# Late hidden tiles' transfers on GpSimd's queue, and split-on-load operands loaded into their own place

## The chip, the cores and the metric

The kernel runs on one core of one Trainium2 chip. The core has five engines that run side by side, each with its own instruction queue: TensorE (PE, matrix products; PEld are its weight loads), VectorE (DVE), ScalarE (ACT), GpSimd (POOL) and SyncE (SP). An engine's queue is worked off in order. DMA transfers are issued from the queues of SP, ACT or POOL and carried out by the core's 16 DMA engines. The metric is the device time of one execution in microseconds (us), smaller is better; the program before takes 2143.97 us (median of 3 runs, 2143.37 to 2144.52).

## The reference

A small hybrid network with two layers over 1024 tokens of 1024 channels, all in fp32. Layer 0 mixes by retention and a gated delta rule, layer 1 by a gated linear recurrence; each layer then has the feed-forward part that the change is in:

```python
def conv_ffn(hn, w_up, conv_w, conv_b, w_down):
    up = causal_dwconv(hn @ w_up, conv_w) + conv_b
    gate, val = jnp.split(up, 2, axis=-1)
    return (jax.nn.silu(gate) * val) @ w_down
...
    for layer in range(DEPTH):
        hn = rms_norm(h, norm_mix[layer])
        ...
        h = h + conv_ffn(rms_norm(h, norm_ffn[layer]), ffn_w_up[layer], ffn_conv_w[layer],
                         ffn_conv_b[layer], ffn_w_down[layer])
    return rms_norm(h, norm_final)
```

The hidden width is 2816, that is 22 tiles of 128 channels, each with a gate and a value part. The convolution is over three tokens, channel by channel.

## The kernel before

**Precision.** PE multiplies a rounded fp32 format. To keep fp32 accuracy every operand is split into a high part (a cast by ScalarE) and a low part (the operand less its high part, by VectorE), and every product is three matmuls, `mm3` (L319 to L321): high by high, high by low, low by high. A weight quarter is 128x512, arrives in a `raw` tile (L292), and is split at L272 (cast, `whi`) and L273 (subtract, `wlo`). Some quarters are sums of others (L294 to L296, L309).

**Seven products for eight.** Pairs of tiles are multiplied by a scheme that needs seven products in place of eight, on sums and differences of blocks. A product (`pair_product`) is 4 blocks of 128 channels deep, so 12 matmuls of 128x128 by 128x512. Operand number o = 0 to 6 has its own place in SBUF, `operand(o)`: 0 to 2 in `s2` (printed as `s_4144` in layer 0), 3 to 6 in `s1` (`s_96`). A place holds the high and the low parts of 4 blocks of 128 channels by 512 tokens.

**First half of the feed-forward, `ffn(layer, gain)` (from L834).** For each of the 22 hidden tiles p, `pair_products` makes gate and value of the tile (seven products, results summed into `halo` at L810). `gate(p)` and `hidden(p)` then apply the convolution (L850 on ACT, two steps L852 on DVE for each of gate and value), the silu (L936) and the product (L941). The tile is needed as an operand of the second half, but the operand places are still in use; so `store_parts(p)` writes its seven operand parts to DRAM. Tiles are grouped by c: 0 to 7, 8 to 15, 16 to 21. Some parts are stored already split (high and low, L880, into `pf_dram`): operands {0, 1, 3} of the first group and {0, 1, 3, 5} of the others. The rest is stored whole (L881, L906, into `sf_dram`), 256 KB each. Tiles of the second half of a group need the tile four (or three) before: they read it back at L894 and L895. In layer 1 the tiles from 16 on are not put through this scheme; they are split at once and stored as two transfers of 512 KB (L870, into `lf_dram`).

**Second half (down-projection).** For c = 0, 1 (and 2 in layer 0), for t = 0 to 3 (256 output channels each), for o = 0 to 6: a product of a weight quarter with operand o of group c, and its eviction into `h` (L820). Group 2 has products of 3 blocks, 9 matmuls.

**Where the operands come from.** `load_set(c, o)` fills place o for group c. A stored-split operand is 8 direct loads (L914). A split-on-load operand is 4 loads of 128x512 (L922) into eight half tiles, its *room*: R and three of the general `t` tiles, used in turn. ACT casts each to the high part in the operand's place (L924), and DVE subtracts into the low part (L925). The sets of the first group are loaded in the course of tile 21's products (`after(21, o)`), each into a place that tile 21's product o has just been the last to read; those of the next group in the last output tile (t = 3) of the group before, by the tables `following` (layer 0) and `plain` (layer 1).

**What sets the order.** Only PE's order of the first two tiles is written by hand. Everything else is laid out per engine by the framework's scheduler from the program and the dependences between tiles. All transfers that are named above are issued by SP, in one order. SP has at most 8 transfers in flight; a transfer whose data or place isn't ready holds up all behind it.

Names for places below: T1 is the passage from tile 21 to group 0 (layer 0), T1' the same in layer 1, T2 from group 0 to group 1 in layer 0, T4 in layer 1, T3 from group 1 to group 2 (layer 0 alone).

Of the kernel before, what the change touches and what calls it, by code (L numbers as in the profile page):

```python
# [16 lines left out]
ALU = mybir.AluOpType  # L17
# [6 lines left out]
HALF = 512  # L24
# [65 lines left out]
def f32(ap):  # L90
    return ap.bitcast(F32)
# [12 lines left out]
class Block:  # L104
# [718 lines left out]
    def ffn(self, layer, gain):  # L823
        nc, I = self.nc, self.I
        V, A = nc.vector, nc.scalar
        third = gain is not None
        sets = 3 if third else 2
        y_dram = self.tc.dram_tile([NPAIR, P, T], F32, name=f"yf_dram{layer}")
        s_dram = self.tc.dram_tile([sets, 5, 4, P, HALF], F32, name=f"sf_dram{layer}")

        p_dram = self.tc.dram_tile([sets, 4, 4, 2, P, HALF], F32, name=f"pf_dram{layer}")
        if not third:
            l_dram = self.tc.dram_tile([NPAIR - 16, 2, P, T], F32, name=f"lf_dram{layer}")
        depth = lambda c: 4 if c < 2 else 3  # L834

        def where(c, o):

            if c == 0 or not third:
                return self.operand(o)
            if c == 1:  # L840
                return self.operand((o + 3) % 7)
            if o < 3:
                i = (20, 14, 26)[o]
                return self.slots1(i, 6).rearrange("p (s n c) -> p n s c", n=2, c=256)
            return self.s2[:, :, 6 * (o - 3):6 * (o - 2), :]
# [10 lines left out]
        blocks = lambda ap: ap.rearrange("p (n j c) -> p n j c", n=2, j=2)  # L856
        halves = lambda ap: ap.rearrange("p (n c) -> p n c", n=2)
        place = {1: 0, 4: 1, 2: 2, 6: 3, 5: 4}

        whole = [{0: 0, 1: 1, 3: 2}] + 2 * [{0: 0, 1: 1, 3: 2, 5: 3}]  # L860
        room, loads = {}, [0, 0, 0]

        def store_parts(p, y, hi):

            hi = hi.bitcast(F32R)
            lo = self.parts.tile([P, T], F32R, tag="lo", name="lo")
            if p >= 16 and not third:
                self.split_half(y, (hi, lo))
                for e, t in enumerate((hi, lo)):
                    nc.sync.dma_start(l_dram[p - 16, e], f32(t))  # L870
                return
            c, k = divmod(p, 8)
            kk = depth(c)
            first = slice(0, HALF)

            def store_split(o, src, at):
                A.copy(halves(hi[:, at]), src)  # L877
                V.tensor_tensor(halves(lo[:, at]), src, f32(halves(hi[:, at])), ALU.subtract)  # L878
                for e, t in enumerate((hi, lo)):
                    nc.sync.dma_start(p_dram[c, whole[c][o], k % kk, e], f32(t[:, at]))  # L880
            store = lambda o, r: nc.sync.dma_start(s_dram[c, place[o], k % kk], r)  # L881
            sub = lambda out, a, b: V.tensor_tensor(halves(out), a, b, ALU.subtract)  # L882
            v = blocks(y)
            t = self.t()
            if k < kk:
                store_split(0, v[:, :, 0], first)
                t1 = t[:, first]
                sub(t1, v[:, :, 1], v[:, :, 0])
                store(1, t1)
                store_split(1, halves(t1), slice(HALF, T))  # L890
                return
            t3, t2 = t[:, 0:HALF], t[:, HALF:]
            t4 = t3
            nc.sync.dma_start(halves(t3), blocks(y_dram[p - kk])[:, :, 1])  # L894
            nc.sync.dma_start(t2, s_dram[c, place[1], k - kk])  # L895
            store_split(3, v[:, :, 1], first)
            sub(t3, v[:, :, 1], halves(t3))
            store(4, t3)
            sub(t2, v[:, :, 1], halves(t2))
            store(2, t2)  # L900
            sub(t4, v[:, :, 0], halves(t2))
            store(6, t4)
            if 5 in whole[c]:
                store_split(5, v[:, :, 0], slice(HALF, T))
            else:
                nc.sync.dma_start(halves(s_dram[c, place[5], k % kk]), v[:, :, 0])  # L906

        def load_set(c, o):

            x, kk = where(c, o), depth(c)  # L910
            if o in whole[c]:
                for k in range(kk):
                    for e in range(2):
                        nc.sync.dma_start(f32(x[:, :, kk * e + k, :]), halves(p_dram[c, whole[c][o], k, e]))  # L914
                return
            if c not in room:
                ts = [self.R] + [self.t() for _ in range(3)][::-1]
                room[c] = [t[:, i * HALF:(i + 1) * HALF] for i in range(2) for t in ts]
            for k in range(kk):
                r = room[c][loads[c] % 8]  # L920
                loads[c] += 1
                nc.sync.dma_start(r, s_dram[c, place[o], k])  # L922
                hi, lo = (x[:, :, e + k, :] for e in (0, kk))
                A.copy(hi, halves(r))  # L924
                V.tensor_tensor(lo, halves(r), f32(hi), ALU.subtract)  # L925

        def load_parts(p):
            places = self.place2(p - 16)
# [1034 lines left out]
```

## Time and profile before

| what | value |
|---|---|
| median of 3 runs | 2143.97 us (2143.37 to 2144.52) |
| profiled execution, its own time | 2145.08 us |
| its span on the core | 2143.2 us |
| granted TensorE clock | 0.999 of full speed |
| PE busy | 2127.4 us, 99% |
| DVE, ACT, POOL busy | 1722.2 us, 1077.3 us, 100.5 us |
| DMA moved | 313.23 MB, mean 146 GB/s |
| SP's queue, share of 16 DMA engines | 42.5% |
| SP's transfers of 256 KB: L914, L922 to t, to R | 136, 67, 17 |

The profile is of one execution by the hardware profiler. A row of the timeline gives start, length, engine (SPq is SP's DMA queue, its length that of the issues), line, operation, output <- input, and count; brackets hold the idle time before it and what ended it. Lengths of one engine's instructions overlap by pipelining, so the distance between starts is what an instruction costs in a row of its like. Names are the tiles' and the DRAM tensors' (`s` is an operand place, `t` a general tile, `h` the residual), without their numbers.

### The profile page before, as it was taken

The numbers are of one execution on the slowest core, as the hardware profiler recorded it, in microseconds if no ns is written. First come the engines' busy times: TensorE is split into PE (matmuls) and PEld (weight loads), VectorE is DVE, ScalarE is ACT, GpSimd is POOL, SyncE is SP. The second block draws the span as 40 slices with busy tenths as digits, with TensorE's granted clock in tenths as the row PEclk, the third lists the DMA queues.
The fourth block names the chain that finished last, engine by engine and source line by source line (L and its number), as shares of the span: only waits on it lengthen the run. The fifth ranks groups of instructions, "written<-read, shape, count | busy, mean of one in ns | idle before, by whom it ended". The sixth has DMA issues, their size and how long they took to land.

```text
span 2143.2 us, 29749 instructions
## 1 busy us (share of the span) xinstructions
PE 2127.4 (99%) x10648; PEld 1771.9 (83%) x10648; DVE 1722.2 (80%) x2630; ACT 1077.3 (50%) x1750; POOL 100.5 (5%) x115
## 2 busy tenths in 40 slices
PE   9999999999999999999999999999999999999998
PEld 7878888888888888887888888888888888888887
DVE  7995677776998989988868786768999889878645
ACT  6444423135665555555324576756655555554222
POOL 0102122300000000000000000000000000000002
PEclk9999999999999999999999999999999999999999
DMA  5354433543145435448745212142354445375542
GB/s 188 91 170 126 136 94 94 172 142 118 46 172 178 160 137 179 172 172 289 233 161 172 72 57 80 64 158 65 123 186 163 149 151 177 118 262 183 182 169 85
DMA packets 242021, 313.23 MB, mean 146 GB/s; under 512 B 62432, under 2 KB 129424, under 8 KB 241872
## 3 DMA queue, kind: packets, MB, share of 16 engines
q1 hardware_dynamic: 205632, 304.15, 42.5%
q10 hardware_dynamic: 35088, 6.36, 1.5%
q8 instruction: 84, 1.38, 0.3%
q0 software_dynamic: 1152, 0.81, 0.2%
q14 instruction: 65, 0.53, 0.1%
HBM read 215.79 MB, written 95.45 MB: 145 GB/s over the span
## 4 chain that ended last, share of the span: by engine, by line
PE 63%; issue 30%; DVE 3%; DMA 2%; POOL 1%; SPq 0%; ACT 0%; POOLq 0%; DVEq 0%
PE ps L319 19%; PE ps L320 18%; PE ps L321 18%; PE pc L319 1%; PE pc L321 1%; PE pc L320 1%; DMA s<-pf_dram 1%; DMA t<-sf_dram 0%; DVE wlo L273 0%; DVE l L1416 0%; DVE l L1418 0%; DVE h L1387 0%; PE pc L1551 0%; PE ps L1595 0%; PE pc L1663 0%
## 5 line engine op out<-in xcount | busy, mean ns | idle before, releaser
L319 PE MATMUL ps<-s,whi 128*128 128x512 f32 (+1 forms) x2692 | 1049.1, 391 | 1.5 <-DVE h L820 0.9
L320 PE MATMUL ps<-s,whi 128*128 128x512 f32 (+1 forms) x2692 | 1044.1, 388 | 2.1 <-DVE s L925 1.9
L321 PE MATMUL ps<-s,wlo 128*128 128x512 f32 (+1 forms) x2692 | 1042.7, 388 | 0.6 <-DVE wlo L273 0.6
L272 ACT CAST whi<-raw 128x512 fp32r<-128x512 f32 (+2 forms) x616 | 374.1, 613 | 611.9 <-PE ps L320 471.6
L319 PEld LDWEIGHTS ps<-s,whi 128*128 128x128 f32 x2692 | 505.8, 188 | 107.0 <-ACT whi L272 1.6
L320 PEld LDWEIGHTS ps<-s,whi 128*128 128x128 f32 x2692 | 505.9, 188 | 106.1 <-DVE s L925 4.6
L321 PEld LDWEIGHTS ps<-s,wlo 128*128 128x128 f32 x2692 | 505.6, 188 | 104.5 <-DVE wlo L273 1.4
L273 DVE TENSOR_TENSOR wlo<-raw,whi 128x512 fp32r<-128x512 f32 (+2 forms) x616 | 415.0, 680 | 50.8 <-ACT whi L272 42.3
L852 DVE SCALAR_TENSOR_TENSOR t<-halo,cols,t 128x1024 f32<-128x1024 f32 x176 | 221.6, 1281 | 2.4 <-ACT t L850 1.0
L820 DVE TENSOR_TENSOR h<-ps,h 128x512 f32<-128x512 f32 x140 | 96.3, 689 | 75.7 <-PE ps L321 75.5
L810 DVE TENSOR_TENSOR halo<-ps,kept 128x512 f32<-128x512 f32 (+1 forms) x138 | 91.8, 666 | 71.1 <-PE ps L321 70.5
L850 ACT ACTIVATE t<-halo,cols 128x1024 f32<-128x1024 f32 x88 | 109.5, 1247 | 18.0 <-DVE halo L810 9.0
L805 ACT COPY kept<-ps 128x512 f32<-128x512 f32 (+1 forms) x138 | 77.0, 558 | 11.0 <-PE ps L321 9.6
L472 POOL TENSOR_TENSOR rtok<-rtok,npow 128x4 f32<-128x4 f32 (+1 forms) x10 | 9.9, 990 | 1097.2 <-DVE rtok L471 1097.2
L877 ACT CAST t<-t 128x512 fp32r<-128x512 f32 x68 | 41.2, 621 | 39.1 <-DVE t L941 37.1
L941 DVE TENSOR_TENSOR t<-t 128x1024 f32<-128x1024 f32 x44 | 53.6, 1219 | 0.0
L553 DVE TENSOR_TENSOR h<-ps,h 128x512 f32<-128x512 f32 (+1 forms) x48 | 28.6, 599 | 30.6 <-PE ps L321 30.5
L882 DVE TENSOR_TENSOR t<-t 128x512 f32<-128x512 f32 x76 | 52.1, 686 | 0.6 <-DMA sf_dram<-t 0.6
L936 ACT ACTIVATE t<-t 128x1024 f32<-128x1024 f32 x44 | 46.8, 1063 | 10.4 <-DVE t L852 10.3
L407 ACT ACTIVATE t<-h 128x512 f32<-128x512 f32 (+1 forms) x49 | 26.9, 564 | 45.8 <-DVE h L553 43.8
L878 DVE TENSOR_TENSOR lo<-t 128x512 fp32r<-128x512 f32 x68 | 46.7, 686 | 0.0
L294 DVE TENSOR_TENSOR raw<-raw 128x512 f32<-128x512 f32 (+1 forms) x64 | 43.6, 681 | 3.3 <-issue 1.9
(341 smaller groups left out, 2170.7 us busy)
## 6 DMA issues: line engine op xcount, KB each, us to landing
raw<-in_ffn_up_dram SPq DMA_DIRECT2D x176, 256.0 KB, 2.7
s<-pf_dram SPq DMA_DIRECT2D x136, 256.0 KB, 5.2
sf_dram<-t SPq DMA_DIRECT2D x84, 256.0 KB, 2.4
pf_dram<-t SPq DMA_DIRECT2D x68, 256.0 KB, 2.6
pf_dram<-lo SPq DMA_DIRECT2D x68, 256.0 KB, 2.6
t<-sf_dram SPq DMA_DIRECT2D x67, 256.0 KB, 4.8
raw<-in_ffn_w_dram SPq DMA_DIRECT2D x64, 256.0 KB, 3.1
raw<-in_mix_in_dram SPq DMA_DIRECT2D x52, 256.0 KB, 3.0
```

The lines of the kernel that those rows point to most:

```text
L272: self.nc.scalar.copy(hi[:, 0:w], raw[:, 0:w])
L273: eng.tensor_tensor(lo[:, 0:w], raw[:, 0:w], f32(hi[:, 0:w]), ALU.subtract)
L319: mm(ps, whi, xhi, start=start, stop=False)
L320: mm(ps, whi, xlo, start=False, stop=False)
L321: mm(ps, wlo, xhi, start=False, stop=stop)
L805: A.copy(kept[o], ps)
L810: V.tensor_tensor(dst(i, j), v(ps), v(kept[k]), ALU.add)
L820: V.tensor_tensor(h(*to[o]), ps.rearrange("p (h c) -> p h c", c=256), h(*to[o]), ALU.add)
L850: A.activation(t, buf[:, 2:2 + T], AF.Identity, scale=w(0), bias=self.col(f"ffn_cb{layer}", tile_i))
L852: V.scalar_tensor_tensor(t, buf[:, 2 + j:2 + j + T], w(j), t, ALU.mult, ALU.add)
L882: sub = lambda out, a, b: V.tensor_tensor(halves(out), a, b, ALU.subtract)
L941: V.tensor_tensor(tg, tg, tv, ALU.mult)
```

## The change

Two things. First, `store_parts` picks its queue by the tile: for p from 16 on all its transfers (stores and the two loads L894, L895) are issued by POOL, else by SP as before. Second, a split-on-load operand is loaded straight into the low part of its own place (as fp32); ACT casts it from there to the high part; DVE subtracts in place. R and the t tiles are not taken, and `room` is gone. Behind the removed lines, lines of the changed kernel are up to 5 lower: L914 stays, the load is L918, the cast L919, the subtract L920.

```diff
@@ -858,16 +858,16 @@
-        room, loads = {}, [0, 0, 0]
 
         def store_parts(p, y, hi):
 
+            queue = nc.gpsimd if p >= 16 else nc.sync
...
             if p >= 16 and not third:
                 self.split_half(y, (hi, lo))
                 for e, t in enumerate((hi, lo)):
-                    nc.sync.dma_start(l_dram[p - 16, e], f32(t))
+                    queue.dma_start(l_dram[p - 16, e], f32(t))
                 return
...
                 for e, t in enumerate((hi, lo)):
-                    nc.sync.dma_start(p_dram[c, whole[c][o], k % kk, e], f32(t[:, at]))
-            store = lambda o, r: nc.sync.dma_start(s_dram[c, place[o], k % kk], r)
+                    queue.dma_start(p_dram[c, whole[c][o], k % kk, e], f32(t[:, at]))
+            store = lambda o, r: queue.dma_start(s_dram[c, place[o], k % kk], r)
...
-            nc.sync.dma_start(halves(t3), blocks(y_dram[p - kk])[:, :, 1])
-            nc.sync.dma_start(t2, s_dram[c, place[1], k - kk])
+            queue.dma_start(halves(t3), blocks(y_dram[p - kk])[:, :, 1])
+            queue.dma_start(t2, s_dram[c, place[1], k - kk])
...
-                nc.sync.dma_start(halves(s_dram[c, place[5], k % kk]), v[:, :, 0])
+                queue.dma_start(halves(s_dram[c, place[5], k % kk]), v[:, :, 0])
 
         def load_set(c, o):
...
-            if c not in room:
-                ts = [self.R] + [self.t() for _ in range(3)][::-1]
-                room[c] = [t[:, i * HALF:(i + 1) * HALF] for i in range(2) for t in ts]
             for k in range(kk):
-                r = room[c][loads[c] % 8]
-                loads[c] += 1
-                nc.sync.dma_start(r, s_dram[c, place[o], k])
                 hi, lo = (x[:, :, e + k, :] for e in (0, kk))
-                A.copy(hi, halves(r))
-                V.tensor_tensor(lo, halves(r), f32(hi), ALU.subtract)
+                nc.sync.dma_start(f32(lo), halves(s_dram[c, place[o], k]))
+                A.copy(hi, f32(lo))
+                V.tensor_tensor(lo, f32(lo), f32(hi), ALU.subtract)
```

The order of instructions moves at the transitions. SP at T1, before: tile 20's and 21's stores and loads stand between the operand loads (`pf_dram` holds the stored-split parts, `sf_dram` the others).

```order
L292 DMA raw<-in_ffn_w_dram 128x512 x3
L914 DMA s_4144<-pf_dram_5168 128x2x256
L894 DMA t<-yf_dram_5166 128x2x256
L895 DMA t<-sf_dram_5167 128x512
L914 DMA s_4144<-pf_dram_5168 128x2x256 x7
L880 DMA pf_dram_5168<-t 128x512
L880 DMA pf_dram_5168<-lo 128x512
L881 DMA sf_dram_5167<-t 128x512 x2
```

And SP at the same place in the change, with all the loads of group 0:

```order
L292 DMA raw<-in_ffn_w_dram 128x512 x4
L914 DMA s_4144<-pf_dram_5168 128x2x256 x16
L918 DMA s_4144<-sf_dram_5167 128x2x256 x4
L914 DMA s_96<-pf_dram_5168 128x2x256 x8
L918 DMA s_96<-sf_dram_5167 128x2x256 x12
L292 DMA raw<-in_ffn_w_dram 128x512 x16
```

The stores have left SP's order, and the 40 operand loads stand in the order of their operands; the later group's split-on-load sets, which stood early in the rooms, stand in the order of the others too.

VectorE at T1, before (L925 is the subtract of a split-on-load operand, L820 an eviction of the down-projection, halo_98 the gate's tile):

```order
L925 TENSOR_TENSOR s_4144<-t,s_4144 128x2x256 x2
L820 TENSOR_TENSOR h_89<-ps,h_89 128x2x256
L925 TENSOR_TENSOR s_4144<-t,s_4144 128x2x256
L820 TENSOR_TENSOR h_88<-ps,h_88 128x2x256 x2
L925 TENSOR_TENSOR s_96<-t,s_96 128x2x256 x3
L925 TENSOR_TENSOR s_96<-R,s_96 128x2x256
L820 TENSOR_TENSOR h_89<-ps,h_89 128x2x256
L925 TENSOR_TENSOR s_96<-t,s_96 128x2x256 x3
L925 TENSOR_TENSOR s_96<-R,s_96 128x2x256
L820 TENSOR_TENSOR h_88<-ps,h_88 128x2x256
L925 TENSOR_TENSOR s_96<-t,s_96 128x2x256 x3
L852 SCALAR_TENSOR_TENSOR t<-halo_98,cols,t 128x1024
```

VectorE in the change, from the first subtract of group 0 on:

```order
L920 TENSOR_TENSOR s_4144<-s_4144 128x2x256 x2
L273 TENSOR_TENSOR wlo<-raw,whi 128x512
L852 SCALAR_TENSOR_TENSOR t<-halo_98,cols,t 128x1024
L920 TENSOR_TENSOR s_4144<-s_4144 128x2x256 x2
L273 TENSOR_TENSOR wlo<-raw,whi 128x512
L820 TENSOR_TENSOR h_88<-ps,h_88 128x2x256
L273 TENSOR_TENSOR wlo<-raw,whi 128x512
L852 SCALAR_TENSOR_TENSOR t<-halo_98,cols,t 128x1024
L852 SCALAR_TENSOR_TENSOR t<-halo_99,cols,t 128x1024
L820 TENSOR_TENSOR h_89<-ps,h_89 128x2x256
```

and directly behind it:

```order
L920 TENSOR_TENSOR s_96<-s_96 128x2x256 x2
L820 TENSOR_TENSOR h_88<-ps,h_88 128x2x256
L920 TENSOR_TENSOR s_96<-s_96 128x2x256 x3
L852 SCALAR_TENSOR_TENSOR t<-halo_99,cols,t 128x1024
L920 TENSOR_TENSOR s_96<-s_96 128x2x256 x6
L820 TENSOR_TENSOR h_88<-ps,h_88 128x2x256
L920 TENSOR_TENSOR s_96<-s_96 128x2x256
L273 TENSOR_TENSOR wlo<-raw,whi 128x512
```

The four convolution steps of tile 21 (halo_98 and halo_99), which stood behind the last subtracts, stand between them now, since the t tiles they write are free. The same order stands in layer 1. On PE the first five matmuls of output tile t = 1 come ahead of operand 6's product of t = 0.

VectorE at T3, before:

```order
L820 TENSOR_TENSOR h_88<-ps,h_88 128x2x256
L273 TENSOR_TENSOR wlo<-raw,whi 128x384
L820 TENSOR_TENSOR h_89<-ps,h_89 128x2x256
L273 TENSOR_TENSOR wlo<-raw,whi 128x384
L294 TENSOR_TENSOR raw<-raw 128x384
L925 TENSOR_TENSOR s_4144<-R,s_4144 128x2x256
L820 TENSOR_TENSOR h_88<-ps,h_88 128x2x256
```

and in the change:

```order
L820 TENSOR_TENSOR h_88<-ps,h_88 128x2x256
L273 TENSOR_TENSOR wlo<-raw,whi 128x384
L920 TENSOR_TENSOR s_4144<-s_4144 128x2x256 x3
L820 TENSOR_TENSOR h_89<-ps,h_89 128x2x256
L273 TENSOR_TENSOR wlo<-raw,whi 128x384
L820 TENSOR_TENSOR h_88<-ps,h_88 128x2x256 x2
```

One subtract stood ahead of the third eviction; three stand ahead of the second now.

## The prediction

> **What bounds the kernel now.** I read the profile from the whole to the part: the busy shares, then the matmuls by stretch of time, then what TensorE (PE) waited for, and only then the queue that feeds it. The page's busy line:
>
> ```profile
> PE 2127.4 (99%) x10648; PEld 1771.9 (83%) x10648; DVE 1722.2 (80%) x2630; ACT 1077.3 (50%) x1750; POOL 100.5 (5%) x115
> ```
>
> PE is the bound, and a change that adds or removes no matmul can only move time that PE loses. "Busy" hides a part of such losses, because matmuls overlap. Two PE rows from the first transition of layer 0 (columns: start, length, engine, line; in brackets idle time and who ended it) show how to see them:
>
> ```profile
> 1002.02 0.39 PE L321 MATMUL ps<-s,wlo 128*128 128x512 f32 x1
> 1002.25 0.39 PE L319 MATMUL ps<-s,whi 128*128 128x512 f32 x1
> 1003.12 0.50 PE L320 MATMUL ps<-s,whi 128*128 128x512 f32 x1 [0.48 <-DVE s L925]
> ```
>
> Matmuls that wait for nothing start 0.227 us apart (1002.25 less 1002.02, rounded); the third starts 0.87 after the second and so lost 0.64, though only 0.48 shows as idle. So I count: a stretch should hold its length divided by 0.227. The windows view (length, then busy time and count of PE, PEld, DVE, ACT, POOL, the granted clock, DMA share, GB/s) around each change of operands:
>
> ```profile
> core 0: us, PE busy (x) PEld busy (x) DVE busy (x) ACT busy (x) POOL busy (x), PEclk, DMA share, GB/s
> 985.00:1012.00 27.00, 23.92 (x96) 16.95 (x95) 18.05 (x28) 14.03 (x22) 0.00 (x0) 1.00 0.94 334
> ...
> 1066.00:1081.00 15.00, 15.00 (x67) 11.98 (x66) 5.77 (x9) 3.73 (x6) 0.00 (x0) 1.00 1.08 389
> ...
> 1912.00:1935.00 23.00, 22.84 (x98) 17.78 (x97) 18.80 (x30) 13.81 (x22) 0.00 (x0) 1.00 0.91 320
> 1985.00:2010.00 25.00, 25.00 (x112) 20.72 (x111) 17.46 (x28) 7.88 (x13) 0.00 (x0) 1.00 0.81 287
> ```
>
> Layer 0, first half to down-projection (**T1**): 96 of 119 matmuls, 27 − 96 × 0.227 = 5.2 us lost. Layer 1, the same place (**T1'**): 23 − 98 × 0.227 = 0.8. The change to the second operand group (**T2** in layer 0, **T4** in layer 1) loses nothing: 67 × 0.227 and 112 × 0.227 fill their windows. At the change to the third group (**T3**, layer 0 alone) two neighbouring rows show one gap:
>
> ```profile
> 1151.02 0.39 PE L321 MATMUL ps<-s,wlo 128*128 128x512 f32 x1
> 1152.33 0.47 PE L319 MATMUL ps<-s,whi 128*128 128x512 f32 x1 [0.92 <-DVE h L820]
> ```
>
> 1.31 − 0.23 = 1.1 us. The places that the change touches thus cost 5.2 + 0.8 + 1.1 = **7.1 us**, 0.33% of the span, and no more than that can be won. What released PE is in its waits (waiting line, releaser, us, times, longest):
>
> ```profile
> PE ps L320 <- DVE s L925: 1.9, 6, 0.5
> ...
> PE ps L319 <- DVE h L820: 0.9, 1, 0.9
> ```
>
> VectorE's subtract of the split-on-load operands (L925) and one eviction queued behind it. Why it is late is seen in SyncE's queue in T1:
>
> ```profile
> 966.34 0.52 SPq L914 DMA_DIRECT2D s<-pf_dram  x1
> ...
> 968.25 4.45 SPq L914 DMA_DIRECT2D s<-pf_dram  x7
> ...
> 977.69 0.53 SPq L914 DMA_DIRECT2D s<-pf_dram  x1
> 980.39 0.32 SPq L881 DMA_DIRECT2D sf_dram<-t  x1
> 980.77 4.46 SPq L914 DMA_DIRECT2D s<-pf_dram  x7
> 985.28 1.54 SPq L922 DMA_DIRECT2D t<-sf_dram  x3
> ```
>
> The second set's eight loads (L914) are cut in two: from 968.25 + 4.45 = 972.7 to 980.8 SP stands behind stores of tile 20, for 8 us with one load. Layer 1, whose late tiles store little, has no such hole:
>
> ```profile
> 1893.12 6.41 SPq L914 DMA_DIRECT2D s<-pf_dram  x10
> ```
>
> **Part 1: the last six tiles' transfers move to POOL.** 42 in layer 0 and 12 in layer 1, in tiles 16 to 21. Before tile 21 PE loses nothing, so only T1 can gain. Their price on POOL: the nearest rows are
>
> ```profile
> L1437 POOL DMA_DIRECT2D l<-t_dram x32 | 17.7, 555 | 84.9 <-DMA t_dram<-l 52.5 <-PE pc L1466 17.0 <-ACT l L1448 14.2
> ...
> l<-t_dram POOLq DMA_DIRECT2D x32, 16.0 KB, 2.4
> l<-t_dram SPq DMA_DIRECT2D x32, 16.0 KB, 2.0
> ```
>
> 0.56 us of POOL per issue, and 0.4 us more to landing. Nine per tile are 9 × 0.56 = 5.0 us of a tile's 19.05 us (84 matmuls × 0.227), and POOL has nothing else to do there, so they hide; if an issue took over 19.05 / 9 = 2.1 us they would not. The Trainium skill warns of that ("SBUF — State Buffer", the "DVE blocks DMA" trap): descriptors of a GpSimd DMA can't be written while VectorE holds a shared port. VectorE is busy for most of this stretch; in the POOL row above nothing of the sort shows, at 16 KB, and no row has POOL issue 256 KB.
>
> What does not leave is the traffic. The Trainium skill puts this as a rule ("DMA: Bandwidth & Descriptors", "Issuing engines are not separate DMA queues"): transfers of all engines interleave on the same 16 DMA engines, and another issuer saves only issue time. The windows agree (334 and 389 GB/s, DMA share 0.94 and 1.08): what is saved is the standing still, not the 256 KB. At 389 GB/s one takes 0.67 us.
>
> **Part 2: loads go into the operand's own place.** No L922 into R and the t tiles any more; cast and in-place subtract instead. Counts stay 16 per group of four. What a cast and a subtract cost before:
>
> ```profile
> L924 ACT CAST s<-t x48: 604/622/626, 990.7 to 1999.3; 128x512 fp32r<-128x512 f32 x48
> ...
> L925 DVE TENSOR_TENSOR s<-t,s x48: 681/685/693, 991.4 to 2001.1; 128x512 fp32r<-128x512 f32 x48
> ...
> 998.88 1.89 DVE L925 TENSOR_TENSOR s<-t,s 128x512 fp32r<-128x512 f32 x3
> ...
> 967.04 2.48 DVE L852 SCALAR_TENSOR_TENSOR t<-halo,cols,t 128x1024 f32<-128x1024 f32 x2
> ```
>
> 0.62 for a cast; 0.69 for a subtract, 0.60 each in a row ((1.89 − 0.69) / 2); the convolution L852 1.20 (2.48 − 1.28). No row shows the subtract in place; it reads and writes as many elements, so 0.60 is my value, between 0.60 and 0.69 (16 × 0.09 = 1.4 us at most per transition). Two things follow. The t tiles are no longer held, so tile 21's four convolution steps come forward into T1 (the order shows them between the subtracts). And a load can't run ahead of PE: it waits until PE has read the place.
>
> **T1, layer 0.** Tile 21's first product frees its first place after three matmuls: 966.34 + 0.52 = 966.9, less 3 × 0.227, so T = 966.2. Set 2's first load is the 17th: 966.9 + 16 × 0.67 + 2.7 (a lone load to landing, below) = 980.3, and eight transfers of tile 20, now beside it, add 8 × 0.67 = 5.4: 985.7.
>
> ```profile
> raw<-in_ffn_up_dram SPq DMA_DIRECT2D x176, 256.0 KB, 2.7
> ```
>
> From there VectorE works through its new order: one cast 0.62, 16 subtracts, three L273 and four L820 at 0.60, four L852 at 1.20, so 23 × 0.60 + 4 × 1.20 = 18.6, and 0.69 for the last L273, the low part of the first weights of the second output tile: 1005.6. PE wants that after 13 products (7 of tile 21, 6 of the first output tile; 12 matmuls, 2.72 us each) and two matmuls: 966.2 + 35.4 + 0.45 = 1002.0. Loss 3.6 in place of 5.2: **−1.6**. Bounds: 3.1 us less if the eight transfers are done in time or VectorE's order is not tight (−4.4, what layer 1 loses now); +1.4 for the dearer subtract.
>
> **T1', layer 1.** Starts at 1893.0. No nine-transfer tile, but two of 512 KB (4 × 0.67 = 2.7): 1893.6 + 10.7 + 2.7 + 2.7 = 1909.7; + 0.62 + 18.6 + 0.69 = 1929.6 if VectorE never idles, about 1930.8 with the 1.2 us that I allow for evictions it has to wait for. PE wants it at 1893.0 + 35.8 = 1928.8: loss 2.0 in place of 0.8: **+1.2** (0 to +2.5). Here the convolution's 4.8 us are new in a stretch that was nearly closed.
>
> **T2 and T4.** Before, eight loads went early into R and the t tiles; the rest ran without a break:
>
> ```profile
> 1050.94 16.00 SPq L914 DMA_DIRECT2D s<-pf_dram  x24
> ...
> 1068.97 5.25 SPq L914 DMA_DIRECT2D s<-pf_dram  x8
> ...
> 1970.37 21.45 SPq L914 DMA_DIRECT2D s<-pf_dram  x32
> ```
>
> 16.00 / 24 = 0.67 each, the DMA's own pace. Now all 44 of T2 stand in one stretch: 44 × 0.67 = 29.5, from 1050.9 to 1080.4, the last landing by 1083.1. That is set 3; counted in PE's new order its product runs 136 to 155 matmuls behind the point where the last output tile begins (1050.2, three matmuls ahead of the first load): 1081.0 to 1085.3. Its eight land one by one from 1078.4, PE reads them half as fast: 2 us of slack, **0** (0 to +2.0). T4 is the same with no store beside it: **0** (0 to +1.5).
>
> **T3.** The last rows before:
>
> ```profile
> 1134.89 9.45 SPq L914 DMA_DIRECT2D s<-pf_dram  x13
> 1144.50 0.48 SPq L922 DMA_DIRECT2D R<-sf_dram  x1
> ...
> 1147.37 0.69 DVE L820 TENSOR_TENSOR h<-ps,h 128x512 f32<-128x512 f32 x1 [0.68 <-PE ps L321]
> ```
>
> The L820 at 1147.37, the second of the third group, stands in the new order behind set 4's three subtracts, whose loads are the 22nd to 24th. The 24th was issued by 1144.3 and lands some 4.9 later (between 2.7 alone and 5.2, the page's median in a full queue): 1149.2. Cast and subtract: 1150.5; L820 ends at 1151.2. The fourth product waits for it and would start at 1151.25 − 9 × 0.227 = 1149.2 (the gap above is in front of the fifth): loss 2.0 in place of 1.1, **+0.9** (−0.5 to +2.5).
>
> **Sum.** −1.6 + 1.2 + 0 + 0.9 + 0 = **+0.5 us** on the profiled execution's 2145.1 (span 2143.2 and 1.9 around it): 2145.6. It lies 1.1 above the runs' median of 2143.97, so for the runs **2144.5**. A measurement tells about 0.2% (4.3 us) from no change, so this is "the same".
>
> **The rivals.** *SP's hole is all there is to T1.* Then layer 0 loses what layer 1 loses now, 0.8, and nothing comes back elsewhere: −4.4, 2139.6; with T1' and T3 gone too, −7.1, 2136.9. For it: the hole of 8 us. Against: VectorE's 18.6 us in one chain and the convolution steps in it. Chance 0.14, of which 0.11 count as faster.
> *Place-bound loads (slower).* Eight loads that were early are now in the stretch at each of T2, T3 and T4, 8 × 0.67 = 5.4 us each. T2's slack is 2 us; it is gone if a load takes 0.67 + 2 / 44 = 0.72 us, or if SP waits for PE's places (8 deep in flight) that long. At 0.80 us it costs 44 × 0.13 − 2 = 3.7 in T2 and as much in T4, with T3's bound of 2.5: about +10, 2154. For it: no row shows loads that are bound to places and at full pace for 44. Against: x32 at 0.67 in T4, into places too. Chance 0.16, of which 0.13 count as slower.
> *The move does nothing*, because the DMA engines and not SP's queue hold T1: the 5.2 stays, 2146.1, chance 0.12, inside "same"; this is what the skill's rule on issuing engines would give.
> *POOL's issues crawl* (over 2.1 us each, the skill's trap): tile 20's data reach memory after their loads need them, T1 grows by 9 × 0.5 or more: +5, 2149, chance 0.03.
>
> **How the numbers follow.** Forecast 0.55 for 2144.5, its own range 2141 to 2148 by the bounds of T1 and T1'. With the rivals: faster 0.11, same 0.73, slower 0.16; 8 in 10 reach from 2140.0 to 2149.5.
>
> **What would show it.** Right: T1 holds about 103 of 119 matmuls, PE waiting for L273 or an L920; SP's L914 rows 16 in a row from 966; T1' about 92 in 23 us; T2 full. Wrong: T1 still 96 (no relief), or 115 (the first rival); gaps in T2 or T4 released by DMA or L920 (the second); POOL's issues above 2 us.

## The result, and the profile after

| | median us | range | runs |
|---|---|---|---|
| before | 2143.67 | 2143.14 to 2144.52 | 4 |
| changed | 2156.77 | 2154.74 to 2157.70 | 4 |

The changed kernel is slower by 13.1 us: ratio 1.0059, 95% interval 1.0042 to 1.0077. The forecast was 2144.5 with a range to 2149.5, and "the same". The profiled execution of the changed kernel took 2157.39 us, its span is 2155.6, which is 12.4 over the span before. The page's busy line after:

```profile
PE 2130.3 (99%) x10648; PEld 1772.8 (82%) x10648; DVE 1722.5 (80%) x2630; ACT 1074.9 (50%) x1750; POOL 130.5 (6%) x169
```

The same matmuls, the same work on VectorE, and 30 us more of POOL, which was idle there. So the 12 us are waits of PE again. The windows view of the changed kernel at the places of the prediction (columns as there), with T1 split into the time before and behind 985:

```profile
978.00:988.00 10.00, 7.58 (x34) 5.95 (x33) 3.79 (x6) 0.62 (x1) 0.54 (x1) 1.00 1.06 395
985.00:1012.00 27.00, 23.03 (x99) 18.02 (x98) 23.49 (x36) 16.76 (x26) 1.28 (x2) 1.00 0.85 306
1066.00:1092.00 26.00, 24.14 (x99) 17.66 (x98) 14.35 (x24) 6.18 (x11) 0.00 (x0) 1.00 0.87 310
...
1917.00:1942.00 25.00, 21.66 (x88) 17.13 (x87) 23.14 (x35) 16.05 (x26) 0.00 (x0) 0.93 0.79 275
2010.00:2024.00 14.00, 12.70 (x55) 9.87 (x54) 9.63 (x16) 5.24 (x9) 0.00 (x0) 1.00 0.56 201
```

Count the matmuls as before: 10 us should hold 44, 27 us 119, 26 us 115, 25 us 110, 14 us 62. T1 holds 99, hardly more than the 96 of before; 978 to 988, where nothing was lost before, lacks 10; T2 lacks 16, T1' 22, T4 7. Also new: at T1' the granted clock is 0.93 (third number from the end). What released PE, in its waits:

```profile
PE ps L319 <- DVE h L820: 5.9, 4, 2.8
...
PE ps L319 <- DVE halo L810: 2.4, 1, 2.4
PE ps L321 <- DVE wlo L273: 1.9, 2, 1.3
...
PE ps L320 <- DVE s L920: 1.6, 3, 1.2
PE ps L319 <- ACT s L919: 0.8, 2, 0.6
```

Nearly all of them are VectorE; the last row is ScalarE's casts at T2. But why VectorE is late differs from place to place, and three views side by side show it for the new gap. VectorE's timeline around 981:

```profile
981.75 0.69 DVE L882 TENSOR_TENSOR t<-t 128x512 f32<-128x512 f32 x1 [4.07 <-DMA sf_dram<-t]
982.36 0.68 DVE L273 TENSOR_TENSOR wlo<-raw,whi 128x512 fp32r<-128x512 f32 x1
982.96 0.69 DVE L309 TENSOR_TENSOR raw<-raw 128x512 f32<-128x512 f32 x1
983.56 0.68 DVE L810 TENSOR_TENSOR halo<-ps,kept 128x512 f32<-128x512 f32 x1
```

L882 writes t4 into the place of t3 and waits 4.07 us until the store of t3 has read it; the eviction L810, for which PE waits 2.4 us, is queued three places behind. The store was issued by POOL at 974.5; the DMA issues of 973 to 983, with the median time to landing at the end:

```profile
s<-pf_dram SPq DMA_DIRECT2D x6, 256.0 KB, 10.1
s<-sf_dram SPq DMA_DIRECT2D x4, 256.0 KB, 9.9
sf_dram<-t POOLq DMA_DIRECT2D x3, 256.0 KB, 7.1
pf_dram<-t POOLq DMA_DIRECT2D x2, 256.0 KB, 6.7
pf_dram<-lo POOLq DMA_DIRECT2D x2, 256.0 KB, 7.7
```

and the same view of the kernel before in that window:

```profile
s<-pf_dram SPq DMA_DIRECT2D x5, 256.0 KB, 4.3
sf_dram<-t SPq DMA_DIRECT2D x3, 256.0 KB, 4.3
pf_dram<-t SPq DMA_DIRECT2D x2, 256.0 KB, 4.6
pf_dram<-lo SPq DMA_DIRECT2D x2, 256.0 KB, 4.3
```

The same stores, which took 4.3 to 4.6 us here before (2.4 to 2.6 over the whole program), take about 7 now, and the operand loads beside them 10 in place of 4.3. The stores got out of SP's queue, and met SP's loads in the DMA engines: at 979.0 the trace has fourteen transfers under way, eight loads of SP and six stores of POOL, where SP alone never has more than eight. At 0.67 us each, fourteen are 9.4 us.

At T1' one wait is followed by something that no wait explains; PE's timeline:

```profile
1921.43 0.39 PE L321 MATMUL ps<-s,wlo 128*128 128x512 f32 x1
1924.59 0.47 PE L319 MATMUL ps<-s,whi 128*128 128x512 f32 x1 [2.77 <-DVE h L820]
...
1925.83 0.63 PE L320 MATMUL ps<-s,whi 128*128 128x512 f32 x1
1926.25 0.63 PE L321 MATMUL ps<-s,wlo 128*128 128x512 f32 x1
```

and the granted clock of these stretches (first number behind POOL's column):

```profile
1921.40:1924.60 3.20, 0.43 (x3) 0.04 (x1) 3.20 (x6) 2.94 (x5) 0.00 (x0) 1.00 1.08 371
1924.60:1928.60 4.00, 4.00 (x11) 3.15 (x12) 4.00 (x6) 2.30 (x4) 0.00 (x0) 0.59 1.08 381
```

2.93 us of standing still, then eight matmuls at 0.43 us instead of 0.227 under a granted clock of 0.59: 1.6 us on top.

**A table by place.** All kernels below have the same 10648 matmuls, so the time from matmul a to matmul b of PE's sequence can be compared with the kernel before. Each number is that time less the one in the profile of before, in us (matmuls 5200 to 5310 for the gap before T1, 5310 to 5450 T1, 5450 to 5850 T2, 5960 to 6150 T3, 9500 to 9660 T1', 9880 to 10030 T4; all is the first to the last). It is from one execution each; the runs of one kernel differ by up to 4.4 us (e3, whose profiled execution is 2.7 over its median), so differences under 1 us in a cell, and under 4 in the last column, say little alone. T1 of e2, e3, e5 and e10 and T1' of the changed kernel and of e10 contain 1.2 to 1.6 us of matmuls at a low granted clock (last section).

| kernel | gap before T1 | T1 | T2 | T3 | T1' | T4 | all |
|---|---|---|---|---|---|---|---|
| changed | 2.7 | −0.8 | 3.7 | −0.7 | 4.4 | 2.0 | 11.4 |
| queue only (e1) | 2.2 | −1.7 | 0.0 | −0.6 | 0.0 | 0.0 | 0.0 |
| own place only (e2) | 0.0 | 2.3 | 2.9 | −0.1 | 1.6 | 2.0 | 8.6 |
| changed, 20 and 21 on SP (e3) | 0.0 | 3.5 | 3.5 | −0.3 | 0.5 | 2.0 | 9.7 |
| changed, convolution late (e4) | 2.2 | −3.2 | 3.7 | −0.6 | 1.6 | 2.0 | 5.9 |
| changed, t4 elsewhere (e5) | 0.0 | 0.9 | 3.8 | −0.1 | 4.2 | 2.0 | 11.1 |
| changed, 8 loads fewer (e6) | 2.0 | −1.2 | 0.3 | −0.8 | 3.8 | 0.0 | 3.8 |
| queue only, t4 elsewhere (e7) | 0.0 | −1.3 | 0.1 | −0.2 | 0.2 | 0.0 | −0.5 |
| mixed (e8) | 0.0 | −1.7 | −0.1 | −0.8 | 0.3 | 0.0 | −2.3 |
| stores behind the loads (e9) | 0.0 | −5.6 | 1.1 | −0.2 | 0.0 | 0.0 | −5.0 |
| changed, ACT's queue (e10) | 0.4 | 1.8 | 4.3 | −0.1 | 3.7 | 2.0 | 11.1 |
| e9, stores in front again (e11) | 0.0 | −0.6 | −0.1 | −1.0 | −0.2 | 0.0 | −2.1 |

### The profile page after: what moved, and what is told of

The parts are those of the page before. It is cut to its first block, busy times and chain, and to the rows that moved or that the text cites. A ratio compares the mean times of both kernels' runs of the same rounds, so it can differ in the third digit from the quotient of the medians.

```text
span 2155.6 us, 29847 instructions
## 1 busy us (share of the span) xinstructions
PE 2130.3 (99%) x10648; PEld 1772.8 (82%) x10648; DVE 1722.5 (80%) x2630; ACT 1074.9 (50%) x1750; POOL 130.5 (6%) x169
## 4 chain that ended last, share of the span: by engine, by line
PE 87%; DMA 4%; DVE 4%; issue 3%; POOL 1%; SPq 0%; ACT 0%; POOLq 0%; DVEq 0%; ACTq 0%
PE ps L319 26%; PE ps L321 26%; PE ps L320 26%; DMA s<-sf_dram 2%; DMA s<-pf_dram 1%; PE pc L319 1%; PE pc L321 1%; PE pc L320 1%; DMA sf_dram<-t 1%; DVE wlo L273 1%; DVE s L920 0%; DVE l L1411 0%; DVE l L1413 0%; DMA l<-gc_dram 0%; PE pc L489 0%
## 5 line engine op out<-in xcount | busy, mean ns | idle before, releaser
L273 DVE TENSOR_TENSOR wlo<-raw,whi 128x512 fp32r<-128x512 f32 (+2 forms) x616 | 414.0, 679 | 47.1 <-ACT whi L272 38.2
L820 DVE TENSOR_TENSOR h<-ps,h 128x512 f32<-128x512 f32 x140 | 96.2, 688 | 78.8 <-PE ps L321 78.5
L810 DVE TENSOR_TENSOR halo<-ps,kept 128x512 f32<-128x512 f32 (+1 forms) x138 | 91.7, 664 | 72.1 <-PE ps L321 71.5
L850 ACT ACTIVATE t<-halo,cols 128x1024 f32<-128x1024 f32 x88 | 109.5, 1246 | 15.6 <-DVE halo L810 11.3
L805 ACT COPY kept<-ps 128x512 f32<-128x512 f32 (+1 forms) x138 | 77.0, 558 | 11.1 <-PE ps L321 9.6
L919 ACT CAST s<-s 128x512 fp32r<-128x512 f32 x65 | 39.1, 619 | 41.3 <-DMA s<-sf_dram 39.5
L882 DVE TENSOR_TENSOR t<-t 128x512 f32<-128x512 f32 x76 | 51.9, 684 | 4.1 <-DMA sf_dram<-t 4.1
L920 DVE TENSOR_TENSOR s<-s 128x512 fp32r<-128x512 f32 x65 | 42.3, 687 | 15.1 <-ACT s L919 14.9
```

Of the source, the lines that this page charges most:

```text
L273: eng.tensor_tensor(lo[:, 0:w], raw[:, 0:w], f32(hi[:, 0:w]), ALU.subtract)
L805: A.copy(kept[o], ps)
L810: V.tensor_tensor(dst(i, j), v(ps), v(kept[k]), ALU.add)
L820: V.tensor_tensor(h(*to[o]), ps.rearrange("p (h c) -> p h c", c=256), h(*to[o]), ALU.add)
L850: A.activation(t, buf[:, 2:2 + T], AF.Identity, scale=w(0), bias=self.col(f"ffn_cb{layer}", tile_i))
```

## The experiments

**The two halves apart (e1, e2).** e1 has `queue` as in the change and `load_set` as before; e2 the reverse:

```diff
-            queue = nc.gpsimd if p >= 16 else nc.sync
+            queue = nc.sync
```

Expected of e1:

> The change's first half alone: transfers of tiles 16 to 21 on POOL, split-on-load operands through R and the t tiles as before. Theory A (the move takes away the order that SP gave: tile 20's stores now share the DMA engines with the operand loads, land late and hold up VectorE): the 2.7 us gap of PE around 981.5 is there, released by L810 behind an L882 that waits for a store; T1 loses 3 to 4.5 of the 5.5 us it lost before; T2, T3, T4 as before (0.2, 1.2, 0). Theory B (the loss sits in the in-place loads alone): no gap before T1, T1 near 1 us, total 2 to 5 us faster than before. By A the total is within 2 us of before, 2142 to 2146.

Measured: 2145.41 us against 2144.07, ratio 1.0007 (0.9998 to 1.0017). Theory A holds: the gap is there (2.2), T1 gets 1.7 back, the rest is as before, and the sum is nothing.

Expected of e2:

> The change's second half alone: loads into the operand's own place, all transfers on SP as before. If the in-place loads cost what the changed kernel lost at T2 (0.2 to 3.6), T4 (0 to 1.8) and most of T1' (1.0 to 5.3), these stand here too and the total is 7 to 10 us over before, 2151 to 2154; no gap around 981.5; T1 5 to 7 us. Rival (POOL's transfers are what slows these places): T2 and T4 lose under 1 us and T1' about 1, total within 2 us of before.

Measured: 2153.08, ratio 1.0041 (1.0025 to 1.0057), 9 us slower. The loads into the own place cost T2 (2.9), T4 (2.0) and T1 (2.3, of which 1.6 are the low clock) by themselves; T1 thus loses some 8 us, over the 5 to 7 expected. Of T1' it is 1.6, so the other 2.8 of the changed kernel come only when both halves are together. VectorE's order differs between the two there: in e2 the first eviction of T1' stands behind four subtracts and one convolution step, in the changed kernel behind these and two weight subtracts (L273).

**Which tiles on POOL (e3).**

```diff
-            queue = nc.gpsimd if p >= 16 else nc.sync
+            queue = nc.gpsimd if 16 <= p < 20 else nc.sync
```

> The changed kernel with tiles 20 and 21 back on SP, 16 to 19 on POOL. Theory A: the gap of 2.7 us around 981.5 goes, since SP again puts tile 20's stores ahead of the loads; T1 loses the 1 to 2 us more that the hole in SP's order costs (5 to 6.5 in place of 4.0), T2, T3, T4 as in the changed kernel, so the total is within 2 us of it, 2154 to 2157. Rival (any use of POOL's queue before T1 costs): the gap stays.

Measured: 2152.14, ratio 1.0038 (1.0024 to 1.0051). The gap goes, as expected. T1 is worse by 4.3 than in the changed kernel, more than the 1 to 2.5 expected (1.6 of it are the low clock), and T1' falls to 0.5, which wasn't expected; the total is 2 us below the expected range. T1' has the order of e2 there, and the third set's first load lands 19.1 us after the first issue of the loads, against 20.3 in e2 and 20.0 in the changed kernel: the 1.1 us between e2 and e3 at T1' are those of the landing.

**The convolution behind the subtracts again (e4).**

```diff
+            if c == 0 and o == 2:
+                held.extend(self.t() for _ in range(3))
+                for t in held:
+                    nc.gpsimd.memset(t[:, 0:4], 0.0)
...
+            if c == 0 and o == 6:
+                for t in held:
+                    nc.gpsimd.tensor_tensor(t[:, 0:4], t[:, 0:4], f32(x[:, 0, 2 * kk - 1, 0:4]), ALU.add)
```

> The changed kernel, with the three t tiles held from the third set's load to the last subtract, as the rooms held them, by 128x4 writes and reads of POOL; tile 21's convolution then stands behind the subtracts again. Nothing is left out. Theory C (the convolution steps ahead of an eviction made T1' lose 2.9 us in one wait, 1.6 us at the lower granted clock behind it, and 0.8 at the end): T1' falls from 5.3 to 1 to 2 us, T1 from 4.0 to 2 to 3; T2, T4 and the gap before T1 stay (3.6, 1.8, 2.7): total 4 to 6 us under the changed kernel, 2150 to 2153. Rival (late landing of the third set, not the order, sets T1 and T1'): both stay within 1 us.

Measured: 2151.75, ratio 1.0035 (1.0021 to 1.0049), 5 us under the changed kernel. Theory C holds: T1' falls from 4.4 to 1.6 over before, and T1 by 2.4. At T1' PE's wait for the first eviction falls from 2.9 to 1.5 (a convolution step is 1.2), and the low clock's 1.6 goes with it; what is left of T1' is half a microsecond more than expected. It is the order on VectorE that makes the price of T1': in the changed kernel the first eviction there stands behind four subtracts, a convolution step and two weight subtracts, all of them queued behind the first cast of the third set; here the convolution is out of the way.

**Where does the gap come from (e5)?** t4 is written into a part of the hidden tile that nothing reads any more:

```diff
-            t4 = t3
...
-            sub(t4, v[:, :, 0], halves(t2))
-            store(6, t4)
+            V.tensor_tensor(v[:, :, 1], v[:, :, 0], halves(t2), ALU.subtract)
+            queue.dma_start(halves(s_dram[c, place[6], k % kk]), v[:, :, 1])
```

> The changed kernel, with the last difference of store_parts written into the half of the hidden tile that is no longer read, in place of over t3, whose store is still under way. Nothing is left out. Theory A (the gap of 2.7 us before T1 is VectorE at L882 waiting until tile 20's store of t3 has been read, because that store now shares the DMA engines with SP's loads): the gap is under 0.3 us, T1 stays at 4.0 within 1 us, the rest as in the changed kernel, total 2.0 to 3.0 us under it. Rival (VectorE or PE is held up there by something else, such as POOL's descriptors): the gap stays above 2 us.

Measured in one execution: 2156.8, in the range of the changed kernel. The mechanism is as said, the gap is gone to the last tenth; its gain isn't there. PE's wait for the first eviction of T1, 2.3 us in the changed kernel (the row at 994.92 below, in the part on the prediction), is 3.95 here, and the low clock stands behind it, 1.6 of the 1.7 us by which T1 is worse (T3 is 0.6 worse, too):

```profile
990.42 0.39 PE L321 MATMUL ps<-s,wlo 128*128 128x512 f32 x1
994.59 0.66 PE L319 MATMUL ps<-s,whi 128*128 128x512 f32 x1 [3.79 <-DVE h L820]
995.06 0.63 PE L320 MATMUL ps<-s,whi 128*128 128x512 f32 x1
```

A wait had been taken away in front of a later one that it was covering in part.

**Count or places at T2 and T4 (e6)?**

```diff
-                    for e in range(2):
+                    for e in range(1 if c == 1 and o < 2 else 2):
```

> The changed kernel without 8 of the 44 operand loads at T2 and at T4: the low parts of operands 0 and 1 of the second group aren't loaded, so the products use what stood there. If the count of loads in one stretch decides (0.67 us each, 8 in flight): everything behind them lands 5.4 us earlier, T2 loses under 1.0 in place of 3.8 and T4 under 0.3 in place of 1.8. Rival (the loads wait for PE to free the places, so their count doesn't matter): T2 and T4 stay within 0.7 us of the changed kernel.

Measured in one execution: 2149.39. T2 falls from 3.7 to 0.3, T4 from 2.0 to 0.0; the windows of this run are full (26 us hold 115, 20 us hold 88):

```profile
1066.00:1092.00 26.00, 25.85 (x114) 21.04 (x114) 19.29 (x32) 7.75 (x14) 0.00 (x0) 1.00 0.68 240
2000.00:2020.00 20.00, 20.00 (x90) 16.57 (x89) 16.26 (x27) 7.59 (x13) 0.00 (x0) 1.00 0.46 162
```

The count of loads decides, not the release of the places.

**Can the move to POOL be made to pay (e7, e8)?** e7 is e1 with the edit of e5. e8 is e7 with own-place loads for layer 0's first group alone, and the t tiles held as in e4.

> The first half of the change alone (POOL's queue for tiles 16 to 21, rooms as before) with the same edit in store_parts. Theory A: the gap before T1 (2.2 us there) goes, T1 keeps its gain of 1.7, T3 0.5, the rest as before: 2.0 to 2.6 us under the kernel before, 2141.4 to 2142.2. Rival (the wait moves on to T1): same as the kernel before within 0.7 us.

> As the kernel with POOL's queue, the rooms and the edit in store_parts, but in layer 0's first group the split-on-load operands go into their own place, with the t tiles held to the last subtract so that tile 21's convolution stays behind. By the terms of the runs so far: gap before T1 0, T1 3.2 less than before, T2 0, T3 -0.6, layer 1 unchanged: 3.5 us under the kernel before, 2140 to 2141.3. Rival (the terms don't add, since the later group's rooms then take the t tiles from the convolution of tile 21): T2 1 to 3 us worse, same as before within 1 us.

Measured: e7 2144.44, ratio 1.0000 (0.9991 to 1.0008); e8 2144.35, ratio 1.0000 (0.9991 to 1.0009). Both expected gains were wrong, and the totals are those of the rivals. The gap goes in both. In e7, of the 2.2 us that it cost in e1, 0.4 come back in T1, 0.4 in T3 and 0.2 in T1'; the rest only makes up for e1's 1.3 over the kernel before (medians; −0.1 in e7). PE's wait for T1's first eviction is 2.8 now, 1.6 in e1, as the rival has it. In e8 T1 gains 1.7 and not 3.2, and T2, where its rival put the loss, is as before, so neither mechanism is right there. In e7:

```profile
990.49 0.39 PE L321 MATMUL ps<-s,wlo 128*128 128x512 f32 x1
993.53 0.47 PE L319 MATMUL ps<-s,whi 128*128 128x512 f32 x1 [2.65 <-DVE h L820]
```

Three kernels (e1, e7, e8) with different waits around T1 end within 1.5 us of the kernel before. What they have in common are 40 loads and seven stores of 256 KB to be moved between 966 and 1000.

**So take the seven stores out of the stretch (e9, e11).** The seven parts of tile 20 belong to the third group, whose first loads (into the rooms) start at 1077.7 in the kernel before, 100 us later, and the rest at 1125.4. e9 has all transfers on SP, own-place loads in layer 0's first group (which leaves the t tiles to tile 20 for longer), the edit of e5, rooms elsewhere, and puts the seven off until the first output tile is done:

```diff
+            late = third and p == NPAIR - 2
+            put = (lambda out, src: waiting.append((out, src))) if late else nc.sync.dma_start
...
+                if (c, t) == (0, 0):
+                    for out, src in waiting:
+                        nc.sync.dma_start(out, src)
```

> All transfers on SP, rooms for the later groups and for layer 1 as before; in layer 0's first group the split-on-load operands go into their own place, and tile 20's seven stores (needed only at T3) are issued after the 40 operand loads and the first weights behind them; store_parts with the edit of before. Theory D (T1 is set by the number of transfers that stand ahead of the operand loads between 966 and 1000, whatever the queue: 40 loads and seven stores): without the seven, 7 x 0.67 = 4.7 us less traffic, no gap before T1, T1 loses 0 to 1.5 of 5.5: 4 to 5.5 us under the kernel before, 2138.8 to 2140.5. Rival (the places' release by PE or VectorE's chain sets T1, as the moved wait in the last two runs might also say): T1 still loses 3 us or more, within 2.5 us of before.

Measured: 2138.70 us (2137.53 to 2140.01, 11 runs) against 2144.16, ratio 0.9975 (0.9966 to 0.9984): 5.5 us faster than the kernel before and 18 faster than the changed one. In the table T1 gains 5.6 and T2 gives back 1.1, for which no run looks for the cause. T1 is full (119 matmuls fill 27 us):

```profile
985.00:1012.00 27.00, 27.00 (x120) 22.22 (x119) 23.70 (x38) 17.51 (x28) 0.00 (x0) 1.00 0.94 335
```

and SP's timeline shows why; the L1000 row is the first of the seven stores:

```profile
968.27 10.07 SPq L918 DMA_DIRECT2D s<-pf_dram  x15
978.50 2.48 SPq L923 DMA_DIRECT2D s<-sf_dram  x4
981.14 5.73 SPq L918 DMA_DIRECT2D s<-pf_dram  x8
987.07 8.02 SPq L923 DMA_DIRECT2D s<-sf_dram  x12
995.26 2.37 SPq L292 DMA_DIRECT2D raw<-in_ffn_w_dram  x4
997.96 0.33 SPq L1000 DMA_DIRECT2D pf_dram<-t  x1
```

e11 is e9 with `late = False`, all else the same:

> The kernel of the last faster run, with tile 20's seven stores back at their own place in SP's queue, after the first set's loads; everything else of it stays (own-place loads in layer 0's first group, the edit in store_parts, rooms elsewhere). Theory D (the seven stores ahead of the loads are what T1 waits for): T1 loses 3 to 7 us again, total 2142 to 2146, that is 4 to 7 us over the run with the stores behind. Rival (the own-place loads or the edit in store_parts make the gain, the place of the stores doesn't matter): within 1 us of it, 2138 to 2140.

Measured: 2144.29, ratio to the kernel before 1.0000 (0.9990 to 1.0010). T1 is back at 98 matmuls, with the second set's loads behind the stores from 978.3 on (SP's timeline and the windows view):

```profile
978.31 5.29 SPq L918 DMA_DIRECT2D s<-pf_dram  x8
...
985.00:1012.00 27.00, 24.47 (x98) 17.46 (x97) 25.01 (x38) 16.26 (x26) 0.00 (x0) 1.00 0.96 343
```

The last of the 40 loads lands at 1004.3, in e9 at 1000.0: 4.3 us, against 7 × 0.67 = 4.7 for the stores. The place of the seven stores makes all of e9's gain; the own-place loads and the edit alone give nothing. Whether putting the stores off pays without these two was not run.

**Is it POOL, or any second queue (e10)?**

```diff
-            queue = nc.gpsimd if p >= 16 else nc.sync
+            queue = nc.scalar if p >= 16 else nc.sync
```

> The changed kernel with ACT's queue in place of POOL's for tiles 16 to 21. Theory A in its plain form (any second queue that lets the stores and the loads run side by side makes the gap): the gap of PE before T1 is 1.5 us or more, T2 and T4 as in the changed kernel, total within 3 us of it. Rival (POOL's transfers take more than their share, 4096 B packets beside SP's 1024 B): the stores of tile 20 land within 5 us, the operand loads beside them within 8, and the gap is under 1 us.

Measured in one execution: 2155.92. Both are half right. With ACT as the issuer the stores land sooner and the loads beside them don't suffer so much, in the same window as above:

```profile
s<-pf_dram SPq DMA_DIRECT2D x5, 256.0 KB, 5.6
s<-sf_dram SPq DMA_DIRECT2D x4, 256.0 KB, 5.8
pf_dram<-t ACTq DMA_DIRECT2D x2, 256.0 KB, 5.0
sf_dram<-t ACTq DMA_DIRECT2D x2, 256.0 KB, 5.3
pf_dram<-lo ACTq DMA_DIRECT2D x1, 256.0 KB, 5.1
```

and the gap is 0.4. So 10 us for a load was seen with POOL as the issuer only. But ACT also issues more slowly: its first six stores take from 976.9 to 983.2, POOL's from 973.9 to 977.1, and at 979.0 eight transfers are under way in place of fourteen. The run does not tell the queue from the pace of issue. And T1 takes up the time (1.8 over before, some 1.4 of it at the low clock), and the total is that of the changed kernel: which queue it is changes where PE waits, not how long.

## Why the prediction was wrong, step by step

**The forecast's bound was right, its sum was not.** PE's spacing, the stretches in which the kernel before loses time and the 7.1 us that could be won all hold; e9 takes 5.5 of them. Three terms failed: the time before T1, put at 0 (2.7 measured), T2 and T4, put at 0 (3.7 and 2.0), and T1', put at +1.2 (4.4). Each left out, or priced too low, a wait for a transfer to land or for an eviction in the middle of VectorE's chain.

**"Before tile 21 PE loses nothing, so only T1 can gain" failed** by 2.7 us, inside tile 21. I counted POOL's issue time (0.56 us measured in the page's row, 0.54 now), found it hidden, and did not ask what waits for a store to be done: L882, and behind it an eviction. The time of an issue was the wrong price; that of a landing, 4.3 us in this window before and 7.1 with the loads beside it, was the right one.

**T1, −1.6 predicted, −0.8 measured.** That the size is near is luck. The wait that I priced, 3.6 us for the last L273, is 1.6; 3.1 stand at two evictions in the middle of VectorE's chain:

```profile
994.92 0.47 PE L319 MATMUL ps<-s,whi 128*128 128x512 f32 x1 [2.15 <-DVE h L820]
...
998.45 0.50 PE L319 MATMUL ps<-s,whi 128*128 128x512 f32 x1 [0.52 <-DVE h L820]
...
1008.66 0.50 PE L321 MATMUL ps<-s,wlo 128*128 128x512 f32 x1 [1.29 <-DVE wlo L273]
```

And the −0.8 holds only together with the gap ahead of T1: without the gap (e5) the first of these waits is 3.95 us and sets off the low clock, and T1 is 0.9 over before. My bound of "3.1 us less" doesn't lead to its −4.4 either, which is 2.8 from −1.6. The reading was half right: SP's hole was real, and closing it brought the loads forward into the same DMA engines. e7, e8 and e11 show that the hole isn't the cause: in e11 the loads resume at 978.3 in place of 980.8, and T1 still loses 27 − 98 × 0.227 = 4.8. That the queue doesn't matter for the total is what e1, e7, e8 and e10 show; I gave it a chance of 0.12, as a rival for T1 alone. The Trainium skill's rule ("DMA: Bandwidth & Descriptors", "Issuing engines are not separate DMA queues") agrees with these runs.

**T2 and T4, 0 predicted, 3.7 and 2.0 measured.** The pace of 0.67 us was right: 44 loads from 1049.8 to 1080.4. The step that failed is the landing, for which I added 2.7 us, the time of a lone load, while the page's row said 5.2 for these loads in a full queue (5.3 measured; eight in flight at 0.67 each are 5.4). At T3 I had used 4.9. At T2 I also looked at set 3 only. Its last load landed at 1085.2 in place of 1083.1, just before the 1085.3 of my own count. (That "PE reads them half as fast" was wrong: 20 matmuls for eight loads are 0.57 us each, a little faster than 0.67.) What PE waited for was set 2, four loads ahead of it in the queue, which must be cast and subtracted besides:

```profile
1076.88 0.62 ACT L919 CAST s<-s 128x512 fp32r<-128x512 f32 x1 [4.95 <-DMA s<-sf_dram]
1078.54 1.90 ACT L919 CAST s<-s 128x512 fp32r<-128x512 f32 x3 [1.04 <-DMA s<-sf_dram]
```

2.4 us are lost at set 2, and 1.1 at two evictions behind it. At T4 1.3 us are lost at a subtract of the last set. This is the rival "place-bound loads", right in its place and direction, and by luck in its price of 3.7 (2.0 at T4), but by the wrong mechanism: e6 shows that the count of loads decides, not SP waiting for places. I gave it 0.16.

**T1', +1.2 predicted, +4.4 measured.** The chain of 18.6 us on VectorE was the right thing to look at, but I followed it to its end only, the last L273 (there PE loses 0.7). The first eviction in the middle of the chain cost 2.9, and the low granted clock behind it 1.6, which no row of before could show. The third set's first load, which I put at 1909.7 (16.6 us after the first issue of the loads), landed 20.0 us after it, at 1917.8; in the kernel before it was 20.1 (1913.2), which could have been read from its trace. So the landing was mis-sized, but is no difference between the kernels (19.1 to 20.3 in e2 to e5 and e10, on whichever queue the stores are). Before, one of that set's four loads had come early into R (cast at 1898.9), and neither a convolution step nor a weight subtract stood ahead of the eviction, which started 3.0 us after the landing (1916.2). In the changed kernel a fourth subtract, the convolution step and two weight subtracts come in front of it (3 × 0.60 + 1.20 = 3.0), and it starts 6.0 us after (1923.8). e2 has two weight subtracts less ahead of it and waits 1.3 us less (2 × 0.60), which also spares it the low clock's 1.6: the 2.8 between them.

**T3, +0.9 predicted, −0.7 measured.** The three subtracts ahead of the second eviction did no harm. T3 gains 0.1 to 1.0 in every run, own-place loads or not; no run looks for the cause, which stays open.

**The sum.** 2.7 − 0.8 + 3.7 − 0.7 + 4.4 + 2.0 = 11.3 of the 12.4 us between the spans; 1.0 more stands behind the last matmul, where the kernels differ by as much without any change there.

## What to carry to other kernels

Another queue moves the issue, not the bytes: where the DMA engines are full (here 380 to 400 GB/s), look for transfers that are not needed yet and put them behind those that are, in the same queue, whose order is then the priority. A staging buffer that lets eight loads run ahead is worth its space if the stretch is closed: removing it puts these loads onto the critical stretch at the full pace each (0.67 us), and a load in a full queue lands 5.3 us after its issue, not 2.7. Where a wait is removed, name the next one in the same stretch and price it; in-order engines must be followed at every eviction in the chain, not at its end alone.

## What was not expected of the hardware

**The granted clock after standing still.** Behind a loss of 2.93 us (changed, T1') and one of 3.95 us (e5) eight matmuls ran at 0.43 us with a granted clock of 0.59 and 0.53, and the same in e10 behind 3.79 (T1) and 2.92 (T1', seven matmuls); behind 2.81 (e7) and 2.91 (e8) none did. In e2, and likewise in e3, it came without a long gap, behind ten microseconds of many small ones:

```profile
990.00:1000.00 10.00, 7.88 (x26) 4.62 (x27) 8.96 (x13) 5.26 (x10) 0.00 (x0) 1.00 1.09 384
1000.00:1004.00 4.00, 4.00 (x12) 3.12 (x11) 2.03 (x4) 3.63 (x6) 0.00 (x0) 0.57 1.09 384
```

(26 of 44 matmuls in the first row.) So a stall of some 3 us can cost half as much again; what exactly sets it off isn't settled. The Trainium skill ("TensorE: Matmul & The Clock Gate", Part 1: The HAM clock gate) gives 426.7 ns between matmuls at half clock and a free-running window of 3413 ns; 0.427 us and eight matmuls (3.4 us) agree with it. That an idle window of about 3.4 us is what throttles is not what e2's rows show; the stalls of 2.92 and 2.93 us are shorter too.

**Transfers in flight.** In the window 973 to 983 of the changed kernel SP's loads took 10.1 us to land beside seven stores of POOL, 5.6 beside five of ACT (e10). Fourteen and eight transfers were under way at 979.0, and at 0.67 us each that is 9.4 and 5.4, so their number accounts for most of both. POOL's stores land in about 7 us beside loads that take 10; that its transfers get more than their share in the DMA engines would explain this rest, but it was not measured by itself.
